# Written order for the second feed-forward product and a stepped final norm in a one-core encoder layer

## The chip, the cores and the metric

The kernel runs on 1 core of one Trainium2 chip. The metric is the device time of one execution in microseconds. Terms used below: TensorE (PE) multiplies matrices and writes to PSUM banks; VectorE (DVE), ScalarE (ACT) and GpSimd (POOL) work elementwise; SyncE (SP) here only starts transfers. Each engine has one queue and works through it in order. A transfer can be started from the queue of SP, ACT or POOL; only POOL's are used to add to what a tile holds.

## The reference

One layer of an encoder over 512 tokens of width 2048: a gated linear recurrence in both directions, differential attention, two gates, and a feed-forward part. The part that the change is about is the end:

```python
x = x + (g_m * branch_m + g_a * branch_a) @ w_out[l]
h2 = _rmsnorm(x, norm2_w[l])
gate, up = jnp.split(h2 @ w_ffn_in[l], 2, axis=-1)
x = x + (jax.nn.silu(gate) * up) @ w_ffn_out[l]      # 512 x 5632 times 5632 x 2048
return _rmsnorm(x, final_norm_w)
```

All of it is in float32.

## The kernel before

**Precision.** TensorE takes each float32 operand as a high and a low part (both of type float32r), and `mm3` issues three matmuls for a product: high by high, high by low, low by high. `split` makes the parts: ScalarE copies the source into the high part (line 149), VectorE subtracts it from the source to give the low part (line 150).

**Seven products for eight.** The large products are cut in 2 x 2 blocks and done by a scheme of seven multiplications with sums and differences of blocks (Strassen's, in Winograd's form). `seven` (line 335) writes one chunk. The inner dimension goes in groups g of 512. For every g the left side has seven factors (X11, S1, S2, X12, S3, S4, X22) and the right side (the weights) seven pieces of 128 x 1024: Q1, Q5, Q6, then Q2, Q3, Q7, then Q4. Some pieces are raw weight blocks, some sums that VectorE makes (lines 348, 356, 362, 369). One piece against one factor is a block of 12 matmuls of 128 x 128 by 512 columns.

**The second feed-forward product** is the chunks fo0 and fo1 (`fo_chunk`, line 1001), 1024 output columns each. The 11 groups of 512 are ten (0 to 9) by the scheme and one plain. The order of the work of a chunk is: first half, g = 0 to 9, each Q1, Q5, Q6 (raw blocks a, b, c); second half, g = 0 to 9, each Q2, Q3, Q7 (raw blocks d, f, e; in the last group f, e, d); the four plain pieces W12, W22, W11, W21, each against two factors; then ten Q4. That is 74 pieces and 78 blocks. Two PSUM banks each (i = 0, 1) of a, b and c collect the products, d those of the plain pieces. Q1, Q2 and the plain ones go to a; Q6, Q7, Q4 to b; Q5, Q3 to c.

**What feeds a block.** `take` (line 206) hands out piece n. Before that, `issue(n + AHEAD)` makes the parts of the pieces up to n + 2 and has `load` start the transfers of raw blocks up to eight further (SP's queue, line 197). There are 3 buffers for high parts, 3 for low parts, and 12 for raw blocks, 6 in a pool of their own and 6 of the 16 in `xpool`, where ten t2 sums live until Q4. The factors of the left side lie in DRAM since the first feed-forward product; `stream` (line 975) lists all 148 in order of use, fetches each with a GpSimd transfer four ahead (line 988) and makes its parts with `factor` (line 452). One such step is taken at each call of `work` (line 326), which `body` makes once per block. These tiles come from a pool of 39, `tpool`.

**After the products.** `post` of `added` (line 808) adds a finished bank into output tiles x of 128 x 512. Q1 gives three scaled copies on ScalarE for each bank (line 813); Q5 (816), Q6 (819), Q7 (821), D (826), Q3 (830), Q2 (834) and Q4 (837) add or subtract on VectorE. The residual x1 is added by a GpSimd transfer that accumulates from DRAM (line 802). `end` calls `final` (line 1002): ScalarE squares the tile and sums along the row (x2j, line 1004), VectorE multiplies by the norm's weight (line 1008) for three of the four tiles of a row block t. With the fourth, the sum of squares (1012) and the power (543, 544) give rstd, and the four tiles are scaled, two on ScalarE (1021), two on VectorE (1017, 1019), and stored (1022). Row blocks 0 and 1 end with Q2 of fo1, 2 and 3 with its Q4.

**What sets the order.** The program writes instructions into a list. `later(ns, fn)` holds a step back until a clock, which `tick` advances by 1296 per half block, has passed. From this list the framework's scheduler makes the five queues: it goes by written order as a priority and by its own estimate of when each operand and buffer is ready, so a queue's order may differ from the written one. Nothing is reordered while the kernel runs.

Of the kernel before, what the change touches and what calls it, by code (L numbers as in the profile page):

```python
# [12 lines left out]
F32 = mybir.dt.float32  # L13
# [7 lines left out]
P = 128  # L21
# [93 lines left out]
def build(ctx, tc, a, out):  # L115
# [12 lines left out]
    def ps(name):  # L128
        return pspool.tile([P, 512], F32, tag="ps", name=name)
# [44 lines left out]
    def parts(name, src, kt):  # L174
        n = src.shape[-1]
        hi = wpool.tile([P, n], F32R, tag="hi", name=f"whi_{name}")
        lo = wpool.tile([P, n], F32R, tag="lo", name=f"wlo_{name}")
        split(src, hi, lo)
        return tuple(w.rearrange("p (k c) -> p k c", k=kt) for w in (hi, lo))

    def chunk(name, srcs, kt, cols, body):
        first = len(pieces)
# [9 lines left out]
    def load(n):  # L192
        while len(raws) <= min(n, len(sources) - 1):
# [3 lines left out]
            nc.sync.dma_start(raw, src)  # L197
            raws.append(raw)

    def issue(n):  # L200
        while len(ready) <= min(n, len(pieces) - 1):
            name, need, make = pieces[len(ready)]
            load(need + (8 if sources[need][2] is not None else 6))
            ready.append(make(name))

    def take(it):
        n = next(it)
        issue(n + AHEAD)
        w = ready[n]
        ready[n] = None  # L210
        return w
# [110 lines left out]


    behind = []

    def work(must=False):
        if behind:
            ready_, fn = behind[0]
            while must and not ready_():
                tasks.pop(0)[1]()  # L330
            if ready_():
                behind.pop(0)
                fn()

    def seven(name, src, order, forms, post, start=None, plain=None, spare=False,
# [73 lines left out]
            add("Q4", g, len(sources) - 1, held(lambda g=g: t2[g]))  # L409

        def body(nm, it):
            bank = {k: [ps(f"{nm}_{k}{i}") for i in range(2)] for k in "abc"}
            last = {b_: n for n, (_, _, to, _) in enumerate(seq) for b_, _ in to}
            begun = set()
            for n, (q_, g, to, posts) in enumerate(seq):
                if start and g == order[0]:
                    start(q_)
                w = take(it)
                for b_, f_ in to:
                    if b_ not in bank:  # L420
                        bank[b_] = [ps(f"{nm}_{b_}{i}") for i in range(2)]
                    while f_ not in forms(g):
                        work(True)
                    hi, lo = forms(g)[f_]
                    for k in range(2):
                        for i in range(2):
                            sl = slice(i * P, (i + 1) * P)
                            mm3(bank[b_][i], [hi[:, k, sl], lo[:, k, sl]],
                                [w[0][:, k], w[1][:, k]], b_ not in begun and k == 0,
                                n == last[b_] and k == 1, skip=True)  # L430
                        yield 6 * MM
                    begun.add(b_)
                    if b_ != to[-1][0]:
                        work()
                for q_ in posts:
                    post(q_, bank)
                if during:
                    during(n)
                work()
# [12 lines left out]
    def factor(name, n, out, f_, src):  # L452

        if n:
            w = x_(f"{name}_{f_}", F32R)
            w = [w[:, :512], w[:, 512:]]
        else:
            w = [t_(f"{name}_{f_}{i}", F32R) for i in "hl"]
        w = tuple(x.rearrange("p (k c) -> p k c", k=2) for x in w)
        split(src, *w)  # L460
        out[f_] = w

    def kept(name, g, out, X, place=lambda n: n < 16):

        def s1():
            X["S"] = half(f"{name}_S")
            V.tensor_tensor(X["S"], X["X21"], X["X22"], ALU.subtract)
            factor(name, place(7 * g + 1), out, "S1", X["S"])

        def s2():  # L470
            V.tensor_tensor(X["S"], X["S"], X["X11"], ALU.subtract)
            factor(name, place(7 * g + 2), out, "S2", X["S"])

        def s3():
            V.tensor_tensor(X["X21"], X["X11"], X["X21"], ALU.subtract)
            factor(name, place(7 * g + 4), out, "S3", X["X21"])

        def s4():
            V.tensor_tensor(X["S"], X["S"], X["X12"], ALU.add)
            factor(name, place(7 * g + 5), out, "S4", X["S"])  # L480

        return ([lambda: factor(name, place(7 * g + 0), out, "X11", X["X11"]), s1, s2],
                [lambda: factor(name, place(7 * g + 3), out, "X12", X["X12"]), s4, s3,
                 lambda: factor(name, place(7 * g + 6), out, "X22", X["X22"])])
# [306 lines left out]
    def added(nm, n, src, final, plain=False):  # L791
# [16 lines left out]
        def post(q_, bank):  # L808
            a_, b_, c_ = (bank[k] for k in "abc")
            for i in range(2):  # L810
# [4 lines left out]
                elif q_ == "Q5":  # L815
                    V.tensor_tensor(x[22, i], x[22, i], c_[i], ALU.add)  # L816
                    G.dma_start(tile_(11, i), src(*place(11, i)))
                elif q_ == "Q6":
                    V.tensor_tensor(x[12, i], x[12, i], b_[i], ALU.subtract)
                elif q_ == "Q7":  # L820
                    V.tensor_tensor(x[22, i], x[22, i], b_[i], ALU.subtract)
                    if not plain:
                        fetch(22, i)
                        later(8000, lambda i=i: end(22, i))
                elif q_ == "D":
                    V.tensor_tensor(x[22, i], x[22, i], bank["d"][i], ALU.add)
                    fetch(22, i)
                    later(8000, lambda i=i: end(22, i))
                elif q_ == "Q3":
                    V.tensor_tensor(x[12, i], x[12, i], c_[i], ALU.add)  # L830
                    fetch(12, i)
                    later(8000, lambda i=i: end(12, i))
                elif q_ == "Q2":
                    V.tensor_tensor(x[11, i], x[11, i], a_[i], ALU.add)
                    end(11, i)
                else:
                    V.tensor_tensor(x[21, i], x[21, i], b_[i], ALU.add)  # L837
                    end(21, i)
        return post

# [81 lines left out]
    def fi_chunk(j):  # L922
# [39 lines left out]

        def start(q_):
            if q_ == "Q4" and j == NFB - 1:
                stream()
        order = (0, 1, 3, 2) if j == 0 else range(4)
        seven(f"fi{j}", lambda g, h_, l: a["w_ffi"][j, g, h_, l], order, lambda g: h2f[g], post,
# [7 lines left out]
    def stream():  # L975
# [20 lines left out]
            fetch(n)  # L996
        for m, g, _ in need:
            fgf[m, g] = {}
        when(lambda: True, [lambda n=n: make(n) for n in range(len(need))])

    def fo_chunk(n):
        def final(t, c, x):
# [4 lines left out]
            if len(mine) < 4:  # L1007
                later(0 if n else 30000, lambda: V.tensor_tensor(x, x, env["fnw"][c], ALU.mult))  # L1008
                tick(0)
                return  # L1010
            ss = sm("ss1", 1)
            V.tensor_reduce(ss, ss3p[:, t * 4:t * 4 + 4], AX.X, ALU.add)
            r = sm("rstd3", 1)
            pow_rstd(r, ss, D, 1)
            for k, (c, x) in enumerate(mine):
                if k == 3:
                    V.scalar_tensor_tensor(x, x, r, env["fnw"][c], ALU.mult, ALU.mult)
                elif k == 2:
# [1 line left out]
                else:  # L1020
                    A.activation(x, x, AF.Copy, scale=r)  # L1021
                (nc.sync if k > 1 else nc.scalar).dma_start(
                    out[t][:, c * 512:(c + 1) * 512], x)

        def start(q_):
            if q_ == "Q4" and n == 0:
# [432 lines left out]
    hm_split()  # L1459
    while chunks:  # L1460
        one()
    tick(1e9)


# [12 lines left out]
```

## Time and profile before

| | us |
|---|---|
| median of 3 runs | 2661.37 (2660.05 to 2668.32) |
| the profiled execution | 2664.15 |
| its span | 2662.4 |
| TensorE busy | 2599.0 (98% of the span) |
| VectorE busy | 2106.5 (79%) |
| ScalarE busy | 1308.8 (49%) |
| GpSimd busy | 253.7 (10%) |

The span runs from the first to the last instruction of the execution. All times in rows are from its start. A matmul's end is modelled from its size and matmuls overlap, so 0.39 us is shown for one where they start 0.23 us apart. PEclk is the mean clock granted to TensorE in a stretch, as a share of full speed. In rows that name a tile, buffer numbers are left out: fo_x is any output tile of fo0 or fo1, whi_fo_Q and wlo_fo_Q the high and low part of any piece, fs_ a streamed factor.

### The profile page before, as it was taken

What the parts mean: (1) busy time and instruction counts of PE and PEld (TensorE: products, weight loads), DVE (VectorE), ACT (ScalarE), POOL (GpSimd) and SP (SyncE); (2) the same over time, 40 slices, a digit from 0 to 9 for tenths busy, and PEclk for the clock granted to TensorE, in tenths of its full rate; (3) what the DMA queues carried; (4) which work ended last, traced back from release to release, by engine and by line L of the source; (5) the groups of instructions that cost most, each with busy time, mean ns of one, the idle gap of its engine ahead of it and who ended that gap; (6) DMA issues with size and microseconds to landing.
All of it is one profiled execution on the core that took longest, in us unless ns stands there. A gap on an engine that the chain in (4) does not pass through costs nothing. (4 is left out here: it accounts for less than half of the span.)

```text
span 2662.4 us, 33245 instructions
## 1 busy us (share of the span) xinstructions
PE 2599.0 (98%) x12184; PEld 2160.8 (81%) x12184; DVE 2106.5 (79%) x2660; ACT 1308.8 (49%) x1848; POOL 253.7 (10%) x448
## 2 busy tenths in 40 slices
PE   7999999999999999998999999999999999999997
PEld 6878888878889988887778888888888878787886
DVE  8977888788875675686788888788888879879885
ACT  8544444545543543354564444444444436646554
POOL 1000000011210122101200000000000001222211
PEclk9999999999999999999999999999999999999999
DMA  7655566744432345447755554565555577777763
GB/s 250 237 187 181 201 200 208 240 119 126 132 104 88 125 158 208 169 150 233 216 203 180 188 195 165 177 211 181 186 190 186 176 281 276 251 256 257 239 224 91
DMA packets 162227, 508.97 MB, mean 191 GB/s; under 512 B 21832, under 2 KB 22120, under 8 KB 162064
## 3 DMA queue, kind: packets, MB, share of 16 engines
q1 hardware_dynamic: 111456, 379.77, 41.6%
q0 software_dynamic: 33712, 97.71, 12.3%
q10 hardware_dynamic: 16896, 29.37, 3.2%
q8 instruction: 95, 1.56, 0.2%
q14 instruction: 68, 0.56, 0.1%
HBM read 445.41 MB, written 50.87 MB: 186 GB/s over the span
## 5 line engine op out<-in xcount | busy, mean ns | idle before, releaser
L145 PE MATMUL aqk_b<-xs,whi_aqk 128*128 128x512 f32 x512 | 161.6, 396 | 0.0
L149 ACT CAST whi_fi_Q<-fi_Q_t 128x1024 fp32r<-128x1024 f32 x88 | 92.5, 1052 | 116.7 <-PE fi_b L145 98.3
L145 PE MATMUL fi_a<-whi_fi_Q,h_X 128*128 128x512 f32 x440 | 147.2, 392 | 0.0
L145 PE MATMUL fi_c<-whi_fi_Q,h_S 128*128 128x512 f32 x440 | 144.6, 390 | 0.0
L145 PE MATMUL fi_b<-whi_fi_Q,h_S 128*128 128x512 f32 x352 | 115.6, 389 | 0.0
L145 PEld LDWEIGHTS aqk_b<-xs,whi_aqk 128*128 128x128 f32 x512 | 94.6, 189 | 18.3
L150 DVE TENSOR_TENSOR wlo_fi_Q<-fi_Q_t,whi_fi_Q 128x1024 fp32r<-128x1024 f32 x88 | 106.2, 1217 | 4.1 <-ACT whi_fi_Q L149 4.1
L362 DVE TENSOR_TENSOR raw_fi_e<-raw_fi_e,raw_fi_f 128x1024 f32<-128x1024 f32 x44 | 53.9, 1224 | 65.0 <-DMA raw_fi_e<-in_w_ffi 64.9
L145 PE MATMUL aqk_b<-xs,wlo_aqk 128*128 128x512 f32 x256 | 100.5, 393 | 0.0
L145 PEld LDWEIGHTS fi_c<-whi_fi_Q,h_S 128*128 128x128 f32 x440 | 82.6, 188 | 17.1
L145 PEld LDWEIGHTS fi_a<-whi_fi_Q,h_X 128*128 128x128 f32 x440 | 82.6, 188 | 16.8
L988 POOL DMA_DIRECT2D fs_X<-fg_X11d x22 | 11.8, 538 | 830.2 <-DVE wlo_fi_Q L150 785.5
L145 PE MATMUL fi_a<-wlo_fi_Q,h_X 128*128 128x512 f32 x220 | 86.0, 391 | 1.9 <-DVE wlo_fi_Q L150 1.8
L348 DVE TENSOR_TENSOR raw_fi_b<-raw_fi_b,raw_fi_a 128x1024 f32<-128x1024 f32 x44 | 53.8, 1223 | 41.5 <-DMA raw_fi_b<-in_w_ffi 36.7
L145 PE MATMUL fi_c<-wlo_fi_Q,h_S 128*128 128x512 f32 x220 | 86.0, 391 | 0.6 <-DVE wlo_fi_Q L150 0.5
L145 PE MATMUL ba_p<-whi_ba,hahl 128*128 128x512 f32 x256 | 82.5, 392 | 0.0
L149 ACT CAST whi_fi_Q<-raw_fi_e 128x1024 fp32r<-128x1024 f32 x44 | 46.4, 1055 | 73.1 <-PE fi_b L145 48.2
L149 ACT CAST whi_fi_Q<-raw_fi_b 128x1024 fp32r<-128x1024 f32 x44 | 46.5, 1056 | 69.5 <-PE fi_c L145 51.9
L145 PE MATMUL bm_p<-whi_bm,hmhl 128*128 128x512 f32 x256 | 80.5, 392 | 0.0
L145 PE MATMUL mqk_b<-xs,whi_mqk 128*128 128x512 f32 x256 | 80.4, 394 | 0.0
L149 ACT CAST whi_fi_Q<-raw_fi_f 128x1024 fp32r<-128x1024 f32 x44 | 46.4, 1055 | 67.4 <-PE fi_c L145 65.3
L145 PEld LDWEIGHTS fi_b<-whi_fi_Q,h_S 128*128 128x128 f32 x352 | 66.1, 188 | 13.6
(837 smaller groups left out, 8452.3 us busy)
## 6 DMA issues: line engine op xcount, KB each, us to landing
raw_fi_a<-in_w_ffi SPq DMA_DIRECT2D x44, 512.0 KB, 3.7
raw_fi_b<-in_w_ffi SPq DMA_DIRECT2D x44, 512.0 KB, 4.2
raw_fi_c<-in_w_ffi SPq DMA_DIRECT2D x44, 512.0 KB, 4.4
raw_fi_d<-in_w_ffi SPq DMA_DIRECT2D x44, 512.0 KB, 4.2
raw_fi_f<-in_w_ffi SPq DMA_DIRECT2D x44, 512.0 KB, 3.8
raw_fi_e<-in_w_ffi SPq DMA_DIRECT2D x44, 512.0 KB, 4.2
raw_aqk<-in_w_aqk SPq DMA_DIRECT2D x32, 512.0 KB, 3.6
raw_fo_a<-in_w_ffo SPq DMA_DIRECT2D x20, 512.0 KB, 4.8
```

The lines of the kernel that those rows point to most:

```text
L145: T.matmul(dst, lhs[l], rhs[r], start=first and i == 0, stop=last and i == 2, skip_group_check=skip)
L149: A.copy(hi, src)
L150: V.tensor_tensor(lo, src, hi.bitcast(F32), ALU.subtract)
L348: V.tensor_tensor(raws[r12], raws[r12], raws[r11], ALU.add)
L362: V.tensor_tensor(raws[r12], raws[r12], raws[r22], ALU.add)
L988: G.dma_start(got[n], fgd[g][f_].rearrange("p (k c) -> p k c", k=2))
```

## The change

From the first block of fo0 to the end, everything is put in a `manual_schedule` region: there each engine issues its instructions in written order. To suit that, the written order changes. A low part is written one piece after its high part: `parts` returns a function for it and `take` calls that one piece ahead (in the region) or as soon as before (outside; there only the order of the low part and of the t2 sum of a Q2 piece changes). A factor's low half is written at the next `work`. `post` is held back by 2000 (two half blocks) in the region. `stream` makes a factor only when it is at most five ahead of the factors used. The last Q4 piece of a chunk goes through its two output banks one after the other instead of in turn. Q4's two additions are written ahead of both `end` calls. The final norm is cut in steps that `later` spreads: for row blocks 0 and 1 by 1300 each, for 2 and 3 by 1. The steps left over are written in their order at the end.

```diff
     def parts(name, src, kt):
         hi = wpool.tile([P, n], F32R, tag="hi", name=f"whi_{name}")
-        lo = wpool.tile([P, n], F32R, tag="lo", name=f"wlo_{name}")
-        split(src, hi, lo)
-        return tuple(w.rearrange("p (k c) -> p k c", k=kt) for w in (hi, lo))
+        A.copy(hi, src)
+
+        def low():
+            lo = wpool.tile([P, n], F32R, tag="lo", name=f"wlo_{name}")
+            V.tensor_tensor(lo, src, hi.bitcast(F32), ALU.subtract)
+            return tuple(w.rearrange("p (k c) -> p k c", k=kt) for w in (hi, lo))
+        return low
...
+    region = []
+
+    def written():
+        if not region:
+            region.append(ctx.enter_context(tc.manual_schedule()))
+
+    def behindhand(fn):
+        if region:
+            later(2000, fn)
+        else:
+            fn()
...
     def take(it):
         n = next(it)
         issue(n + AHEAD)
+        while lows[0] < min(len(ready), n + (2 if region else 3)):
+            ready[lows[0]] = ready[lows[0]]()
+            lows[0] += 1
...
     def work(must=False):
+        if low_parts:
+            low_parts.pop(0)()
         if behind:
...
         def body(nm, it):
+            if nm == "fo0":
+                written()
...
+                used[0] += len({(g, f_) for _, f_ in to} - met)
+                met |= {(g, f_) for _, f_ in to}
                 w = take(it)
...
-                    for k in range(2):
-                        for i in range(2):
+                    for h_ in range(2):
+                        for j in range(2):
+                            k, i = (j, h_) if plain and n == len(seq) - 1 else (h_, j)
...
                 for q_ in posts:
-                    post(q_, bank)
+                    behindhand(lambda q_=q_: post(q_, bank))
...
     def factor(name, n, out, f_, src):
-        split(src, *w)
-        out[f_] = w
+        A.copy(w[0], src)
+
+        def low():
+            V.tensor_tensor(w[1], src, w[0].bitcast(F32), ALU.subtract)
+            out[f_] = w
+        if region:
+            low_parts.append(low)
+        else:
+            low()
...
                     V.tensor_tensor(x[21, i], x[21, i], b_[i], ALU.add)
+            if q_ == "Q4":
+                for i in range(2):
                     end(21, i)
...
-        when(lambda: True, [lambda n=n: make(n) for n in range(len(need))])
+        for n in range(len(need)):
+            when(lambda n=n: n < used[0] + 5, [lambda n=n: make(n)])
...
         def final(t, c, x):
-            ss = sm("ss1", 1)
-            V.tensor_reduce(ss, ss3p[:, t * 4:t * 4 + 4], AX.X, ALU.add)
+
             r = sm("rstd3", 1)
-            pow_rstd(r, ss, D, 1)
-            for k, (c, x) in enumerate(mine):
+
+            def scale():
+                ss = sm("ss1", 1)
+                V.tensor_reduce(ss, ss3p[:, t * 4:t * 4 + 4], AX.X, ALU.add)
+                pow_rstd(r, ss, D, 1)
+
+            def put(k):
+                c, x = mine[k]
...
+            step = 1300 if t < 2 else 1
+            later(step * (1 + t % 2), scale)
+            for k in (0, 3, 1, 2):
+                later(step * (3 + 4 * (t % 2) + (0, 2, 3, 1)[k]), lambda k=k: put(k))
...
-    tick(1e9)
+    while tasks:
+        tasks.pop(0)[1]()
```

## Rows read from the trace of the kernel before

**Rows 1.** Windows: width, busy (x count) of PE, PEld, DVE, ACT, POOL; PEclk, DMA share, GB/s

```profile
2290.00:2372.00 82.00, 78.89 (x342) 63.38 (x341) 73.24 (x83) 49.77 (x67) 20.51 (x39) 1.00 0.89 312
2372.00:2421.50 49.50, 46.40 (x199) 36.93 (x199) 34.40 (x42) 21.52 (x34) 11.05 (x18) 1.00 0.70 218
...
2507.00:2616.00 109.00, 107.52 (x472) 88.04 (x472) 86.01 (x96) 59.40 (x79) 25.21 (x43) 1.00 0.68 215
2616.00:2652.00 36.00, 31.94 (x132) 25.41 (x130) 19.03 (x27) 16.29 (x27) 1.12 (x2) 0.95 0.16 58
sum 445.40, PE 432.57 PEld 351.76 DVE 372.09 ACT 248.50 POOL 88.77; mean PE 72.09 PEld 58.63 DVE 62.02 ACT 41.42 POOL 14.79
```

**Rows 2.** Tiles fo_a, fo_b (min/median/max ns, first to last start) and one chain piece

```profile
L145 PE MATMUL fo_a<-whi_fo_Q,fs_X11h x80: 389/389/477, 2206.6 to 2506.6; 128*128 128x512 f32 x80
...
L145 PE MATMUL fo_b<-whi_fo_Q,fs_X22l x80: 387/389/628, 2398.6 to 2651.7; 128*128 128x512 f32 x80
...
2516.58 2.72 PE fo_c L145 x12
```

**Rows 3.** Waits of TensorE from 2180 on: us in total, times, longest

```profile
PE fo_b L145 <- DVE wlo_fo_Q L150: 4.6, 8, 0.8
```

**Rows 4.** Waits of VectorE, SP's timeline 2478 to 2500, one piece of the chain

```profile
DVE raw_fo_e L362 <- DMA raw_fo_e<-in_w_ffo: 11.4, 9, 2.8
...
2479.66 1.46 SPq L197 DMA_DIRECT2D raw_fo_d<-in_w_ffo  x2
2485.41 0.33 SPq L197 DMA_DIRECT2D raw_fo_e<-in_w_ffo  x1
2490.34 0.33 SPq L197 DMA_DIRECT2D raw_fo_f<-in_w_ffo  x1
2494.35 0.33 SPq L197 DMA_DIRECT2D raw_fo_e<-in_w_ffo  x1
...
2494.35 5.02 DMA raw_fo_e<-in_w_ffo
```

**Rows 5.** Timelines of ScalarE and VectorE around 2400: start, us, what, idle before

```profile
2395.77 0.63 ACT L1004 ACTIVATE x2j<-fo_x 128x512 f32<-128x512 f32 x1 [7.24 <-DMA fo_x<-x1d]
...
2401.51 1.23 DVE L150 TENSOR_TENSOR wlo_fo_Q<-fo_Q_t,whi_fo_Q 128x1024 fp32r<-128x1024 f32 x1 [9.48 <-ACT whi_fo_Q L149]
```

**Rows 6.** Timelines of ScalarE and TensorE around 2630, and a window after it

```profile
2629.23 2.94 ACT L149 CAST whi_fo_Q<-fo_Q_t 128x1024 fp32r<-128x1024 f32 x3 [0.41 <-ACT fo_x L1021]
...
2630.33 0.73 PE L145 MATMUL fo_b<-whi_fo_Q,fs_X22h 128*128 128x512 f32 x2 [3.53 <-ACT whi_fo_Q L149]
...
2631.00:2636.00 5.00, 4.47 (x13) 3.54 (x13) 2.80 (x3) 1.43 (x3) 0.00 (x0) 0.66 0.27 101
```

**Rows 7.** VectorE's timeline in fo0's first half; tile fo_x: the scalings of Q1

```profile
2221.05 0.68 DVE L150 TENSOR_TENSOR fs_S1l<-fs_S,fs_S1h 128x512 fp32r<-128x512 f32 x1
2221.66 1.21 DVE L150 TENSOR_TENSOR wlo_fo_Q<-raw_fo_a,whi_fo_Q 128x1024 fp32r<-128x1024 f32 x1
2222.79 0.68 DVE L150 TENSOR_TENSOR fs_S2l<-fs_S,fs_S2h 128x512 fp32r<-128x512 f32 x1
...
L813 ACT ACTIVATE fo_x<-fo_a x12: 593/612/647, 2284.0 to 2509.2; 128x512 f32<-128x512 f32 x12
```

**Rows 8.** Tile x1d from 2200 on: its transfers

```profile
DMA to landing us min/median/max: 3.9/5.5/8.3
```

**Rows 9.** Tile fo_x: last additions and stores; ScalarE's timeline from 2652 on

```profile
L837 DVE TENSOR_TENSOR fo_x<-fo_x,fo_b x4: 680/685/689, 2432.3 to 2652.1; 128x512 f32<-128x512 f32 x4
...
L1022 ACTq DMA_DIRECT2D out<-fo_x x8: 338/338/375, 2626.2 to 2657.3; - x8
...
2653.87 1.33 ACT L1021 ACTIVATE fo_x<-fo_x,rstd 128x512 f32<-128x512 f32 x2 [0.35 <-POOL rstd L544]
```

**Rows 10.** Waits of GpSimd from 2200 on; tile fs_S: its transfers

```profile
POOL fs_X L988 <- DVE fs_S4l L150: 24.2, 9, 4.2
...
DMA to landing us min/median/max: 2.8/4.9/10.7
```

More of the change, by code (lines that the diff above doesn't have):

```diff
@@ L198, in load @@
             raws.append(raw)
+    region = []
[7 more added lines that the diff above has]
+            fn()
+    lows = [0]
     def issue(n):
@@ L324, in build @@
     behind = []
+    used = [0]
+    low_parts = []
     def work(must=False):
+        if low_parts:
+            low_parts.pop(0)()
         if behind:
@@ L414, in body @@
             begun = set()
+            met = set()
             for n, (q_, g, to, posts) in enumerate(seq):
@@ L459, in factor, with flush @@
         w = tuple(x.rearrange("p (k c) -> p k c", k=2) for x in w)
-        split(src, *w)
-        out[f_] = w
+        A.copy(w[0], src)
[6 more added lines that the diff above has]
+            low()
+    def flush():
+        while low_parts:
+            low_parts.pop(0)()
     def kept(name, g, out, X, place=lambda n: n < 16):
@@ L470, in s2 @@
         def s2():
+            flush()
             V.tensor_tensor(X["S"], X["S"], X["X11"], ALU.subtract)
@@ L478, in s4 @@
         def s4():
+            flush()
             V.tensor_tensor(X["S"], X["S"], X["X12"], ALU.add)
@@ L964, in start @@
             if q_ == "Q4" and j == NFB - 1:
+                used[0] = -4
                 stream()
```

## The prediction, made before the change was run

> **What bounds the kernel now.** The page's engine shares put TensorE far ahead, so only its stalls can be won. The diff gives written order from the second feed-forward product (chunks fo0 and fo1) to the end, so I cut that stretch into windows and compared each width with TensorE's busy time [rows 1]. It idles 3.1 us in fo0's second half, 3.1 us around fo0's last pieces, 1.5 us in fo1's second half and after, and 4.1 us in fo1's last pieces. In all 445.4 - 432.6 = 12.8 us are idle, so the two first halves, which are not shown, are nearly dense.
>
> The loss is larger than the idle time. A block of twelve matmuls takes 2.72 us in a dense run [rows 2]. Each chunk has 78 blocks (70 of the seven products, 8 of the W pieces), so the two need 156 x 2.72 = 424.3 us. From the first fo matmul at 2206.6 to the last at 2651.7 there are 445.1 us [rows 2], and eight transposes in between cost about 1. So about **20 us** are lost: the 12.8 us of idle time, the restarts (a matmul after a wait shows 0.39 us where the dense rate is 2.72/12 = 0.23), and slow matmuls below.
>
> The waits say what comes late. Eight waits of the b bank's matmuls are for a low part, wlo_fo_Q, 0.8 us at most [rows 3]. Behind these VectorE waits 11.4 us for raw_fo_e to land [rows 4]. That transfer is late because its buffer was spoken for: the loads went out as d, d, e, f, e, where the pieces are used d, f, e [rows 4]; the e of 2494.35 went out just before its use, and the chain of waits runs through its 5.02 us [rows 4]. Around fo0's last pieces ScalarE stands still for 7.24 us ahead of a square, x2j, whose operand is still being accumulated by a transfer; the next whi_fo_Q stands behind four squares, and VectorE's low part waits 9.48 us for it [rows 5]. In fo1's last pieces six squares and four scalings of the final norm stand ahead of a whi_fo_Q, which starts at 2629.23; TensorE waits 3.53 us, then runs at a granted share of 0.66 (part of it at 1.2 instead of 2.4 GHz) over the next 5 us [rows 6].
>
> **The change, part by part.**
>
> *Loads in written order.* No instruction is added. SP then loads d, f, e in order of use, each ten pieces before its product. Five of the six buffers of either pool are taken by such a lead, and the sixth came free some three pieces earlier, so a raw piece has about 20 us to land where the late one took 5.02 [rows 4]. The waits for raw_fo_e and raw_fo_f go, and with them the idle time of fo0's second half and part of fo1's.
>
> *Low parts one piece ahead in place of two.* VectorE's order within a step becomes sum for piece n+2, low part of n+1, posts, low half of a factor. Back to back, a low part occupies it 1.13 us and a factor half 0.61 [rows 7]; a sum has the low part's shape, so I price it alike. Three pieces with their two sums and three halves need 5 x 1.13 + 3 x 0.61 = 7.5 us, against 3 x 2.72 = 8.16 of TensorE: it keeps up, with 8% spare. The high part of n+2 may start when block n-1 has freed its buffer; about 1.0 us later (three in a row take 2.94) [rows 6] the low part may follow, and it is wanted two blocks after that start: 5.44 - 1.0 - 1.13 = 3.3 us of slack, as before.
>
> *Where written order still bunches work.* (a) At the change from a chunk's first half to its second, ScalarE gets six scalings of 0.62 [rows 7] among its copies, and VectorE four additions of 0.6. Walking both queues from the end of the last Q1 block (0): the high part of Q2 ends at 1.1, the scalings at 4.4, the next two high parts at 6.0 and 7.6; VectorE does two additions (to 4.1), a half (5.6), a sum (6.7), a low part (7.9), two additions (9.2), a half and a sum (11.0), and the low part of Q7 (12.1). That is wanted at 4 x 2.72 + 0.2 = 11.1: a stall of 1.0, twice. (b) In fo1's Q4 pieces four multiplications by fnw, chained to squares, and two additions are written between two low parts; the second ends at 7.2 where 5.6 was wanted: 1.5. (c) At fo0's start the tail of the first product is unchanged: 0.6. With 0.3 per restart that is about **5 us left**.
>
> *Squares.* They are now emitted seven half-blocks after their transfer. In real time that is W11 and W21 (10.9 us) and a high part (1.1) after W22's end, so 12 us. The transfers start within 3 us of that end and take 3.9 to 8.3 us [rows 8], so they land 7 to 11 us after it. I take no wait. Bounds: nothing, or the 7.24 us again, of which 3.1 us of idle time [rows 1] and about five restarts of 0.3 reached TensorE, 4.6 in all. The Trainium skill (Perfetto Trace Analysis, Tensor Engine Instruction) calls the queues of ACT, DVE and GpSimd strict FIFO: an entry not ready holds all behind it. The rows of the squares agree. By that rule one late transfer brings the old stall back, which is rival B.
>
> *Final norm in steps.* For rows 0 and 1 the reductions and scalings are spread over ten half-blocks of fo1's Q4; 4 x (0.7 + 0.34) = 4.2 us of ScalarE [rows 9] lie in 13.6 us, where the copies leave about 5 idle. The stall there goes: 4.1 us idle [rows 1], 1.7 from 5 us at 0.66 [rows 6] and two restarts, 6.4 in all.
>
> *The tail.* From the last addition (2652.1) to the end are 10.3 us [rows 9]. The last piece now finishes one output tile half a block early, so its addition and square are done when the other tile ends, and the second reduction no longer stands behind scalings: about 1 us earlier. Against this, each ScalarE scaling (0.67 apart now) has its transfer's issue written right behind it, so four scalings and four issues run one by one: 1.7 + 4 x 1.1 = 6.1 us after the last bank, where the last issue now ends 5.5 after it [rows 9]. I take +0.3, ends -0.7 and +0.8. The Trainium skill (Perfetto Trace Analysis, DMA Instruction, HWDGE) has the sequencer wait for such an issue's semaphore before it goes on; no row shows an issue between two scalings, and without that rule the tail would be 0.5 shorter.
>
> *Before the region.* Only the order of low part and sum in Q2's pieces changes. The sum needs no high part and about fits in the wait for it (1.0 us against 1.13), so nothing; if the cover is gone, the nearest row is a short wait for a low part, 0.8 us, a few times. I take 0, ends -3 and +3.
>
> *Sum.* 20 - 5 = 15 lost microseconds return, less 0.3 of the tail and rounded down to **14** for small stalls not walked. The profiled execution took 2664.15 us (span 2662.4), 2.8 above the median of 2661.37; it would take about 2650.2, and the median 2661.37 - 14 = **2647.4**.
>
> **The rivals.**
>
> *A, the forecast* (0.62): 2644 to 2653.
>
> *B, the wait moves* (0.16): squares or a factor's copy still stand ahead of high parts in ScalarE's written order. For it: 5.5 us is the median transfer, 8.3 the longest [rows 8]. Against: the later emission. The 4.6 us of the squares and three more stalls of 1.0 stay: 14 - 7.6 = 6.4 gained, 2655.
>
> *C, slower* (0.10): the factor stream is now held to five ahead, so a fetch is emitted four steps, 10.9 us, before its copy. GpSimd waits up to 4.2 us for a buffer, and a transfer lands in 4.9 us typically, 10.7 at worst [rows 10]. If the sum passes 10.9, ScalarE waits, and all behind it. It decides from 14/148 = 0.1 us per factor on; at 0.25 us it costs 37, and the median would be 2684. Against: 4.2 + 4.9 = 9.1 leaves 1.8 us, and fewer factors alive leave more buffers free.
>
> *D, it does nothing* (0.04): the waits were the transfers' rate, not their order; 2661. For it: a DMA share of 0.89 in fo0's second half [rows 1]. Against: 0.68 in fo1's, with the same loads.
>
> *E, all stalls go* (0.08): 20 less, 2641.
>
> **How the numbers follow.** A change of 0.3% (8 us) is about what a measurement here can tell. A, E and the better part of B lie below 2653.4: 0.74. The rest of B and D lie within it: 0.16. C gives 0.10. The range runs from E's 2641 less one to D with its 3 us, 2640 to 2664.
>
> **What would show it.** Right: loads in the order d, f, e; no wait of VectorE for raw_fo_e; the chain of waits almost all TensorE; no stall over 1.5 us from fo0 on; granted clock 1.00 to the last block; a tail of about 10.6 us. Wrong: ScalarE waiting for transfers (x2j or fs tiles), idle time of TensorE in the first halves, or VectorE never waiting while TensorE does.

## The result, and the profile after

| | before | after |
|---|---|---|
| median, four runs each on the same chip (us) | 2660.71 (2657.53 to 2668.32) | 2642.15 (2639.95 to 2643.95) |
| the profiled execution; its span | 2664.15; 2662.4 | 2642.52; 2639.6 |
| first and last fo matmul start | 2206.6, 2651.7 | 2198.6, 2628.8 |
| from the first to the last: **the stretch** | 445.1 | 430.3 |
| of it, beyond the dense pitch of matmuls: **lost** | 19.2 | 5.1 |
| last fo matmul to the end: **the tail** | 10.72 | 10.75 |

"Lost" sums what the steps from one matmul's start to the next take beyond the dense 0.227 us, over the steps that are longer by more than 0.05.

The changed kernel is faster: ratio 0.9926 (95% interval 0.9911 to 0.9940), 18.6 us by the medians where 14 were forecast. The traces say where it comes from. Their spans differ by 2662.4 - 2639.6 = 22.8 us. Of these the stretch gives 445.1 - 430.3 = 14.8, and the tail nothing. The remaining 2206.6 - 2198.6 = 8.0 us lie ahead of fo0, where all five engines have the same instructions in the same order in both kernels, but for some two dozen of VectorE's and nine of SP's in the last 26 us; 7.0 of the 8.0 are there before these.

The windows over the same parts of the work as in [rows 1] (their edges do not fall on exactly the same matmuls), from fo0's second half on; the columns are those of [rows 1]:

```profile
2282.00:2364.00 82.00, 81.42 (x359) 67.09 (x359) 77.67 (x85) 47.52 (x61) 19.98 (x38) 1.00 0.93 319
2364.00:2413.50 49.50, 49.50 (x221) 40.96 (x220) 32.08 (x38) 26.16 (x42) 13.20 (x22) 1.00 0.54 160
2413.50:2498.00 84.50, 83.19 (x367) 68.60 (x366) 81.77 (x92) 51.31 (x71) 17.00 (x31) 1.00 0.76 268
2498.00:2600.00 102.00, 101.42 (x447) 83.64 (x447) 86.74 (x96) 52.96 (x68) 22.17 (x39) 1.00 0.69 219
2600.00:2628.60 28.60, 27.56 (x121) 22.44 (x120) 19.58 (x28) 17.09 (x29) 2.52 (x3) 1.00 0.23 83
```

Width less TensorE's busy time is 0.6, 0.0, 1.3, 0.6 and 1.0 us. Around fo0's last pieces nothing is idle any more, and the granted clock is 1.00 up to the last block. The DMA share of fo0's second half rose from 0.89 [rows 1] to 0.93 while its idle time went from 3.1 to 0.6: the rate of the transfers was not the limit there, so rival D's reason falls.

The waits of TensorE in the stretch, and VectorE's three largest up to the last fo matmul (us in total, times, longest):

```profile
PE fo_b L145 <- DVE wlo_fo_Q L181: 2.2, 3, 1.0
PE fo_c L145 <- DVE wlo_fo_Q L181: 1.3, 1, 1.3
```

```profile
DVE wlo_fo_Q L181 <- ACT whi_fo_Q L177: 23.6, 32, 3.0
DVE fs_X22l L497 <- ACT fs_X22h L494: 13.1, 6, 3.0
DVE fo_x L1059 <- ACT x2j L1055: 4.9, 1, 4.9
```

VectorE waits for no transfer at all; the 11.4 us for raw_fo_e [rows 4] are gone. Its largest wait is now for ScalarE's high parts, 23.6 us in 32 waits, but TensorE waits only four times for a low part, 3.5 us in all. These four, from its timeline (start, us, what, idle before and its releaser):

```profile
2288.00 0.50 PE L145 MATMUL fo_b<-wlo_fo_Q,fs_S3h 128*128 128x512 f32 x1 [0.58 <-DVE wlo_fo_Q L181]
...
2425.61 0.50 PE L145 MATMUL fo_c<-wlo_fo_Q,fs_S1h 128*128 128x512 f32 x1 [1.31 <-DVE wlo_fo_Q L181]
...
2502.64 0.50 PE L145 MATMUL fo_b<-wlo_fo_Q,fs_S3h 128*128 128x512 f32 x1 [0.58 <-DVE wlo_fo_Q L181]
...
2607.35 0.50 PE L145 MATMUL fo_b<-wlo_fo_Q,fs_X22h 128*128 128x512 f32 x1 [1.04 <-DVE wlo_fo_Q L181]
```

The shown matmul runs on 0.39 us into the idle time, so from start to start these are 0.97, 1.70, 0.97 and 1.43 us instead of 0.23: 0.74, 1.47, 0.74 and 1.20 beyond the pitch. The first and third are the changes of halves, the fourth is fo1's Q4, all where the prediction put them. The second, at fo1's start, it did not have.

### The profile page after: what moved, and what is told of

Read it like the earlier page. It is cut to its first block, busy times and chain, and to the rows that moved or that the text cites. A ratio compares the mean times of both kernels' runs of the same rounds, so it can differ in the third digit from the quotient of the medians.

```text
span 2639.6 us, 33237 instructions
## 1 busy us (share of the span) xinstructions
PE 2590.0 (98%) x12184; PEld 2158.8 (82%) x12184; DVE 2106.2 (80%) x2660; ACT 1308.3 (50%) x1848; POOL 255.1 (10%) x448
## 3 DMA queue, kind: packets, MB, share of 16 engines
q0 software_dynamic: 33712, 97.71, 12.1%
## 4 chain that ended last, share of the span: by engine, by line
PE 77%; DVE 10%; DMA 6%; issue 4%; ACT 2%; POOL 0%; ACTq 0%; DVEq 0%; SPq 0%; POOLq 0%
PE fi_b L145 12%; PE fi_c L145 8%; PE fi_a L145 8%; PE fo_b L145 6%; PE aqk_b L145 5%; PE fo_a L145 4%; PE fo_c L145 4%; PE mqk_b L145 3%; PE bm_p L145 3%; PE ba_p L145 3%; PE mv_p L145 3%; PE ga_b L145 2%; PE gm_b L145 2%; PE ga_a L145 1%; PE ga_c L145 1%
## 5 line engine op out<-in xcount | busy, mean ns | idle before, releaser
L145 PEld LDWEIGHTS aqk_b<-xs,whi_aqk 128*128 128x128 f32 x512 | 94.1, 188 | 17.9
L145 PEld LDWEIGHTS fi_c<-whi_fi_Q,h_S 128*128 128x128 f32 x440 | 83.0, 189 | 17.3
```

What stands on the lines that cost most here:

```text
L145: T.matmul(dst, lhs[l], rhs[r], start=first and i == 0, stop=last and i == 2, skip_group_check=skip)
```

## The experiments

Each kernel was profiled once; "total" is its median (six runs for x1 and x9) or single time. First fo matmul, stretch, lost and tail are measured as in the table above.

| run | total | first fo | stretch | lost | tail |
|---|---|---|---|---|---|
| x1 the changed kernel again | 2646.98 | 2207.1 | 430.3 | 5.2 | 10.75 |
| x2 before, SP alone in written order | 2655.41 | 2200.6 | 442.3 | 16.9 | 10.73 |
| x3 before, all engines in written order | 2723.69 | 2199.2 | 510.8 | 83.8 | 11.98 |
| x4 after, ordered by the scheduler | 2665.19 | 2205.4 | 447.3 | 21.3 | 10.75 |
| x5 after, SP ordered by the scheduler | 2647.09 | 2204.3 | 430.3 | 5.1 | 10.75 |
| x6 after, low part beside high part | 2708.00 | 2202.4 | 493.1 | 65.6 | 10.76 |
| x7 after, norm not in steps | 2659.03 | 2206.7 | 438.7 | 13.6 | 11.81 |
| x8 after, squares early | 2648.44 | 2205.1 | 430.8 | 5.7 | 10.76 |
| x9 after, fnw spread, stores from SP | 2644.46 | 2206.0 | 428.3 | 3.1 | 10.76 |
| x10 after, posts not held back | 2644.40 | 2197.3 | 434.3 | 9.1 | 10.75 |
| x11 after, short factor stream | 2652.05 | 2208.2 | 431.3 | 6.0 | 10.80 |
| x12 after, old order of the tail | 2645.12 | 2200.3 | 430.3 | 5.1 | 10.97 |

Where four of the kernels lose it (us, by first half, second half, and plain pieces with Q4 of each chunk):

| | fo0 first | fo0 second | fo0 rest | fo1 first | fo1 second | fo1 rest |
|---|---|---|---|---|---|---|
| before | 0.72 | 4.53 | 4.46 | 0.99 | 2.29 | 6.18 |
| after | 0.55 | 0.85 | 0 | 1.58 | 0.85 | 1.31 |
| x2 | 2.12 | 1.10 | 3.58 | 0.78 | 2.46 | 6.84 |
| x4 | 0.77 | 8.16 | 9.13 | 0 | 3.03 | 0.17 |

**Is the part ahead of fo0 chance?** x1 is the changed kernel, unaltered.

> The changed kernel once more. Of the 22.8 us between the two traces, 14.9 lie between the first and the last fo matmul (445.1 to 430.3) and 8.0 ahead of the first (2206.6 to 2198.6), where all five queues are the same instruction by instruction. Theory: the 8.0 are chance, the stretch is the change. Then the stretch is 430 again within 1 us, the first fo matmul lies anywhere from 2196 to 2208, and the ratio is 0.993 to 0.995. Rival: the program ahead of fo really became faster (buffers, semaphores); then the first fo matmul is at 2198 or 2199 again and the ratio stays at 0.9926 or below.

Measured: ratio 0.9930 (0.9910 to 0.9950), six runs against eleven. The stretch is 430.3 again, while the first fo matmul starts at 2207.1 instead of 2198.6. Over the runs of the table that start spreads from 2197.3 to 2208.2, with the same instructions ahead of it up to the last 26 us or so. So the 8.0 us are chance in the main; single totals carry about 11 us of it, and the experiments are judged by stretch and tail. One thing stays open. By the means the total falls by 19.8 us in the runs of the result and by 17.9 in those of x1, 3 to 5 more than the stretch. The intervals are wide (16 to 24 and 13 to 24 us), but the kernel before was traced only once, so whether its stretch is always 445 us is not known; the stretch of the changed kernel came as 430.3 in both its traces.

**The order of the loads, or of the other engines?** x2 takes the kernel before and puts SP alone in written order:

```diff
         def body(nm, it):
+            if nm == "fo0":
+                ctx.enter_context(tc.manual_schedule(
+                    engines={mybir.EngineType.SP}))
```

> The kernel before, with SP's queue alone in written order from fo0 on. Theory (order of the loads): the waits for raw_fo_e and raw_fo_f go, and the 3.1 us of idle time of fo0's second half with some 2 of fo1's; squares and norm stay late. First to last fo matmul about 440 of 445. Rival (rate of the transfers): 444 to 446, with VectorE still waiting for raw_fo_e.

x5 is the opposite: the changed kernel, whose region holds every engine but SP.

```diff
-            region.append(ctx.enter_context(tc.manual_schedule()))
+            region.append(ctx.enter_context(tc.manual_schedule(engines={
+                mybir.EngineType.PE, mybir.EngineType.Activation,
+                mybir.EngineType.DVE, mybir.EngineType.Pool})))
```

> The changed kernel with SP left to the scheduler: its loads go out in another order (d, f, d, f, e, d, e, f at the start of a second half), the other four queues as written. With SP alone in written order the waits for raw_fo_e stayed, and the sum of e and f stood 25 us ahead of its use in VectorE's queue, against 2.5 in the changed kernel. Theory (the place of the sum, not the order of the loads, made the late wait): first to last fo matmul 430 to 431, no wait of VectorE for raw_fo_e or raw_fo_b over 1 us. Rival (the order of the loads): 432 to 436, with such waits back.

x2 loads in the order d, f, e, and VectorE still waits for the transfers; its stretch, 442.3, lies between the two expectations. Its waits in x2:

```profile
DVE raw_fo_b L348 <- DMA raw_fo_b<-in_w_ffo: 13.0, 7, 3.5
DVE raw_fo_e L362 <- DMA raw_fo_e<-in_w_ffo: 9.7, 7, 4.2
```

x5's loads are out of order, d, f, d, e (SP's timeline in x5):

```profile
2461.68 0.58 SPq L201 DMA_DIRECT2D raw_fo_d<-in_w_ffo  x1
2469.93 0.33 SPq L201 DMA_DIRECT2D raw_fo_f<-in_w_ffo  x1
2474.81 0.33 SPq L201 DMA_DIRECT2D raw_fo_d<-in_w_ffo  x1
2475.19 0.42 SPq L201 DMA_DIRECT2D raw_fo_e<-in_w_ffo  x1
```

Yet no wait for a transfer is among VectorE's, and the stretch is 430.3. In sum the order of the loads is worth the 2.8 us of x2 (one trace each), and nothing once the rest is in order. The mechanism of the prediction holds in one place: in fo0's second half x2 wins back 3.4 of the 3.7 us that the change does. In fo1's it wins nothing, with a wait of 4.2 us there, and fo0's first half loses 1.4 more. So the order of the loads is not what the waits rest on. What differs between the kernels with them and those without, the tile raw_fo_e shows: the load, the sum of e and f, and the copy that uses the sum (durations, then first and last start), before:

```profile
L197 SPq DMA_DIRECT2D raw_fo_e<-in_w_ffo x20: 327/328/423, 2241.3 to 2558.0; - x20
L362 DVE TENSOR_TENSOR raw_fo_e<-raw_fo_e,raw_fo_f x20: 1212/1225/1228, 2252.9 to 2561.7; 128x1024 f32<-128x1024 f32 x20
L149 ACT CAST whi_fo_Q<-raw_fo_e x20: 1043/1048/1057, 2290.1 to 2583.6; 128x1024 fp32r<-128x1024 f32 x20
```

and after:

```profile
L201 SPq DMA_DIRECT2D raw_fo_e<-in_w_ffo x20: 327/328/1197, 2249.5 to 2537.9; - x20
L390 DVE TENSOR_TENSOR raw_fo_e<-raw_fo_e,raw_fo_f x20: 1214/1217/1219, 2281.5 to 2562.9; 128x1024 f32<-128x1024 f32 x20
L177 ACT CAST whi_fo_Q<-raw_fo_e x20: 1052/1056/1057, 2282.9 to 2565.4; 128x1024 fp32r<-128x1024 f32 x20
```

Before, the first sum stands 37 us ahead of its use, the last 22; after, 1.4 and 2.5. Over all twenty, paired one to one, the median is 25.4 before and 2.5 after, and from a load's issue to its sum 5.3 against 27.1 us. In x2 they are 25.1 and 6.2, in x5 2.5 and 26.7. So the loads were not late for the product. The sum stands about 5 us behind its load's issue, close to where the transfer lands (median 4.4 us, at most 8.9), and low parts that TensorE wants soon stand behind it. VectorE's timeline before, and the matmul that waited:

```profile
2499.46 1.23 DVE L362 TENSOR_TENSOR raw_fo_e<-raw_fo_e,raw_fo_f 128x1024 f32<-128x1024 f32 x1 [2.81 <-DMA raw_fo_e<-in_w_ffo]
2500.61 1.22 DVE L150 TENSOR_TENSOR wlo_fo_Q<-fo_Q_t,whi_fo_Q 128x1024 fp32r<-128x1024 f32 x1
...
2501.88 0.50 PE L145 MATMUL fo_b<-wlo_fo_Q,fs_S2h 128*128 128x512 f32 x1 [0.60 <-DVE wlo_fo_Q L150]
```

That the engines' order other than SP's does it is shown; that it is this place in VectorE's queue is read from the waits and leads of four traces, since no run moves the sum alone.

x4 asks for the rewritten program without the region:

```diff
-            region.append(ctx.enter_context(tc.manual_schedule()))
+            region.append(None)
```

> The changed text, without the region: low parts, held posts, stream limit? no: those that hang on the region fall back to the form of before, the stream's limit, the stepped norm and the tail stay, and the scheduler orders all queues. Theory: loads are out of order again and squares late, the norm's stall (6.4) is gone: first to last fo matmul about 438, VectorE waiting for raw_fo_e. Rival (the text does it, the region nothing): 430 to 432.

Here the expectation described the edit wrongly in part: since the list is not empty, low parts one piece ahead, held posts and the limit of the stream stay as well, and only the ordering falls to the scheduler. It gives 447.3: the rewritten text alone gains nothing in sum. The old waits are back, VectorE's 12.1 us for raw_fo_e and ScalarE's 16.1 us for accumulated tiles. The steps of the norm work here too: from fo1's plain pieces on 0.2 us is lost, where it was 6.2 before. But fo0's second half and last pieces lose 17.3 instead of 9.0, with one wait of 3.74 us.

**The low part in a second step.** x3 gives the kernel before the region and no rewriting; x6 writes the changed kernel's low part right behind its high part.

```diff
         def body(nm, it):
+            if nm == "fo0":
+                ctx.enter_context(tc.manual_schedule())
```

> The kernel before, with every engine in written order from fo0 on and the text not rewritten. Theory (region and rewriting both needed): loads cured, but posts stand right behind their block and the final norm in one piece ahead of a copy, so first to last fo matmul 436 to 440. Rival 1 (the region does it all): 430 to 432. Rival 2 (posts at once hold up VectorE every time): over 445.

```diff
-        while lows[0] < min(len(ready), n + (2 if region else 3)):
+        while lows[0] < min(len(ready), n + 3):
```

> The changed kernel with the low part of a piece written right behind its high part, as before, and all else as in the change. The region alone took 510.8 us from first to last fo matmul. Theory (the low part in a second step is what makes written order pay): behind a sum the low part must wait some 1.1 us for ScalarE's copy; 40 of the sums per chunk, with two waits to three pieces, need 7.5 + 2.2 = 9.7 us where TensorE needs 8.16, so 40 to 60 us more: 470 to 490. Rival (the region alone lost by its posts and the norm in one piece): 430 to 436.

The region alone costs 510.8 - 445.1 = 65.7 us, far more than was expected (436 to 440; the rival of over 445 had put it on the posts). Without the second step the changed kernel takes 493.1 - 430.3 = 62.8 us more. VectorE's timeline in fo0's first half of x6 shows why, and under it one row of ScalarE's:

```profile
2244.10 1.23 DVE L181 TENSOR_TENSOR wlo_fo_Q<-raw_fo_b,whi_fo_Q 128x1024 fp32r<-128x1024 f32 x1 [1.19 <-ACT whi_fo_Q L177]
2245.24 0.68 DVE L497 TENSOR_TENSOR fs_S2l<-fs_S,fs_S2h 128x512 fp32r<-128x512 f32 x1
2245.84 1.22 DVE L384 TENSOR_TENSOR fo_Q_t<-raw_fo_b,raw_fo_c 128x1024 f32<-128x1024 f32 x1
2248.25 1.23 DVE L181 TENSOR_TENSOR wlo_fo_Q<-fo_Q_t,whi_fo_Q 128x1024 fp32r<-128x1024 f32 x1 [1.19 <-ACT whi_fo_Q L177]
...
2254.14 1.23 DVE L181 TENSOR_TENSOR wlo_fo_Q<-raw_fo_b,whi_fo_Q 128x1024 fp32r<-128x1024 f32 x1 [1.19 <-ACT whi_fo_Q L177]
```

```profile
2247.17 1.05 ACT L177 CAST whi_fo_Q<-fo_Q_t 128x1024 fp32r<-128x1024 f32 x1 [2.58 <-DVE fo_Q_t L384]
```

The sum ends, ScalarE copies it, and VectorE stands still for that copy, because the low part is its next instruction; ScalarE in turn stands still while VectorE is on its way to the next sum. Three pieces take 2254.14 - 2244.10 = 10.04 us, where TensorE's three blocks take 8.16. VectorE's work alone was 7.5 in the prediction; the two idle times of 1.19 bring it to 9.9.

**The written steps one at a time.** x10 calls `post` at once, x8 has the squares of accumulated tiles follow at the next tick, x7 writes the final norm in one piece:

```diff
-                    behindhand(lambda q_=q_: post(q_, bank))
+                    post(q_, bank)
```

> The changed kernel with each post written right behind its last block, not two half blocks later. Theory: VectorE reaches the post about a block before TensorE is done with the bank and waits with the next low parts behind it; a few posts per chunk, each eating 1 to 2 us of 3 us of slack: 432 to 436 from first to last fo matmul, the stalls at the change of halves grown. Rival (the slack takes it all): 430 to 431.

```diff
-                        later(8000, lambda i=i: end(22, i))
+                        later(1 if region else 8000, lambda i=i: end(22, i))
...
-                    later(8000, lambda i=i: end(22, i))
+                    later(1 if region else 8000, lambda i=i: end(22, i))
...
-                    later(8000, lambda i=i: end(12, i))
+                    later(1 if region else 8000, lambda i=i: end(12, i))
```

> The changed kernel with the squares of the accumulated tiles written one half block after their transfer is started, in place of seven. Theory: ScalarE stands still until the transfer has landed (7 to 11 us after W22 in fo0) and the high parts of the Q4 pieces stand behind it: a stall of 1 to 4 us in fo0, less in fo1, so 431 to 435. Rival (the high parts ahead of it are enough, the distance was not needed): 430 to 431.

```diff
-            later(step * (1 + t % 2), scale)
-            for k in (0, 3, 1, 2):
-                later(step * (3 + 4 * (t % 2) + (0, 2, 3, 1)[k]), lambda k=k: put(k))
+            scale()
+            for k in range(4):
+                put(k)
```

> The changed kernel with the final norm of a row block written in one piece again. Theory: ScalarE gets two squares, two waits for rstd, four scalings and four issues (about 7 us) ahead of the next high part, which has 3 us of slack: a stall of 3 to 4 us in fo1's Q4 pieces and slow matmuls after it, so 434 to 437 from first to last fo matmul, granted clock under 1 near the end. Rival (any order hides it): 430 to 431.

Posts at once cost 434.3 - 430.3 = 4.0 us, nearly all in one place. VectorE does wait 12.3 us for the d banks in x10, but TensorE has no stall there. The loss is at fo1's start: Q4's additions wait for the b bank, then six multiplications by the norm's weight stand ahead of a low part. VectorE's timeline in x10, and TensorE's:

```profile
2411.08 0.69 DVE L884 TENSOR_TENSOR fo_x<-fo_x,fo_b 128x512 f32<-128x512 f32 x1 [1.61 <-PE fo_b L145]
...
2417.65 3.70 DVE L1059 TENSOR_TENSOR fo_x<-fo_x,fnw 128x512 f32<-128x512 f32 x6
...
2424.28 0.80 PE L145 MATMUL fo_a<-wlo_fo_Q,fs_X11h 128*128 128x512 f32 x1 [2.47 <-DVE wlo_fo_Q L181]
```

The 4.0 are thus the price of early posts together with this block of six; what posts alone cost no run shows. The squares' distance is worth 0.5. ScalarE waits 9.2 us for accumulated tiles in x8, as much as the 9.3 of the kernel before, but in eight waits of at most 2.7 us where before it was two of up to 7.2; all but 0.5 is hidden. The steps of the norm are worth 8.4 in the stretch and 1.1 in the tail, more than the 4 to 7 expected. x7 has the old stall back, longer: TensorE's timeline there, and two windows behind it.

```profile
2622.02 0.79 PE L145 MATMUL fo_b<-wlo_fo_Q,fs_X22h 128*128 128x512 f32 x1 [7.50 <-DVE wlo_fo_Q L181]
2622.61 0.63 PE L145 MATMUL fo_b<-whi_fo_Q,fs_X22l 128*128 128x512 f32 x1
```

```profile
2622.00:2626.60 4.60, 4.58 (x11) 3.63 (x12) 3.74 (x5) 3.51 (x5) 0.00 (x0) 0.54 0.67 260
2626.60:2631.00 4.40, 4.40 (x21) 3.63 (x20) 2.72 (x4) 3.03 (x4) 0.00 (x0) 1.00 0.00 0
```

After 7.5 us of idle time the granted clock is 0.54 (nearly all at 1.2 of 2.4 GHz) for 4.6 us, in which 11 matmuls start; at the dense pitch it would be 20. That is about 2 us on top of the stall.

**The factor stream.** x11 moves towards rival C: the stream three ahead in place of five, its fetches two ahead in place of four.

```diff
-            when(lambda n=n: n < used[0] + 5, [lambda n=n: make(n)])
+            when(lambda n=n: n < used[0] + 3, [lambda n=n: make(n)])
...
-            fetch(n + 4)
+            fetch(n + 2)
```

> The changed kernel with the factor stream cut to three ahead and its fetches to two ahead of their copy. For rival C of the prediction (the shorter stream makes ScalarE wait): a fetch then leads by about two blocks, 5.4 us, where a transfer takes 4.9 typically and 10.7 at worst, so ScalarE waits at many of 148 factors and the stretch grows to 440 or more. Against it: the factor's three steps of lead still hide most, 430 to 434; then rival C was far off.

It costs 1.0 us in all. With half the lead four fetches come late, and ScalarE waits 9.0 us for them, 3.3 at most, but nearly all of it is hidden; at the lead of the change no such wait is left. Rival C had no footing.

**The tail, and a version that might beat both.** x12 takes back the order of the two output banks and the additions ahead of `end`. x9 spreads fo0's and fo1's multiplications by fnw over half blocks and issues all stores from SP.

```diff
-                            k, i = (j, h_) if plain and n == len(seq) - 1 else (h_, j)
+                            k, i = h_, j
...
-            if q_ == "Q4":
-                for i in range(2):
-                    end(21, i)
+                    end(21, i)
```

> The changed kernel with the last piece's two output banks in turn again and each end right behind its addition. Theory: the stretch stays at 430.3; the first addition can start 0.7 us later against the last matmul, so square and rstd of the first row block come 0.7 later, and the tail grows from 10.75 by 0.5 to 0.7. Rival (the serial scalings and issues on ScalarE set the tail): within 0.2 of 10.75.

```diff
-                later(0 if n else 30000, lambda: V.tensor_tensor(x, x, env["fnw"][c], ALU.mult))
+                spread[0] += 1
+                later(2600 if n else 12000 + 2592 * spread[0],
+                      lambda: V.tensor_tensor(x, x, env["fnw"][c], ALU.mult))
...
-                (nc.sync if k > 1 else nc.scalar).dma_start(
+                nc.sync.dma_start(
```

> The changed kernel with three edits for what is left: fo0's multiplications by the norm's weight spread over its Q4 pieces (six in a row, 3.7 us, stood ahead of the low part of fo1's fourth piece: a stall of 1.5), fo1's written two half blocks later (a stall of 1.2), and all stores started from SP, so that ScalarE's four last scalings run back to back. Theory: first to last fo matmul 430.3 less 2.5, 427.8; tail 10.75 less 1.2, 9.5; ratio to the kernel before 0.992, 3 to 4 us under the changed kernel. Rival for the tail (the landing of the last store sets it, wherever it is started): tail 10.5 or more.

x12's tail is 10.97, so the reordering is worth 0.2 us, not the 0.5 to 0.7 expected. x9's stretch is 428.3, the shortest of all: the stall at fo1's start is gone, the one in fo1's Q4 fell from 1.43 to 0.79. Its ratio, 0.9923 (0.9907 to 0.9938), can't be told from the 0.9930 of x1. Its tail did not move, where 9.5 was expected. ScalarE's timeline at the end of the changed kernel:

```profile
2630.86 0.72 ACT L1077 ACTIVATE fo_x<-fo_x,rstd 128x512 f32<-128x512 f32 x1 [0.15 <-POOL rstd L591]
2631.61 0.34 ACTq L1078 DMA_DIRECT2D out<-fo_x  x1
2631.99 0.72 ACT L1077 ACTIVATE fo_x<-fo_x,rstd 128x512 f32<-128x512 f32 x1 [0.42 <-ACT fo_x L1077]
...
2635.02 0.36 ACTq L1078 DMA_DIRECT2D out<-fo_x  x1
```

ScalarE's and SP's timelines at the end of x9:

```profile
2636.33 2.69 ACT L1079 ACTIVATE fo_x<-fo_x,rstd 128x512 f32<-128x512 f32 x4 [0.15 <-POOL rstd L591]
...
2637.08 4.46 SPq L1080 DMA_DIRECT2D out<-fo_x  x8
```

And all of x9's stores in the view of the output (ns min/median/max, first and last start):

```profile
L1080 SPq DMA_DIRECT2D out<-fo_x x16: 332/384/604, 2615.2 to 2640.9; - x16
```

With an issue between them, scalings start 2631.99 - 2630.86 = 1.13 us apart; in x9 four take 2.69. The Trainium skill (Perfetto Trace Analysis, DMA Instruction, HWDGE) says that the sequencer is free for its next instruction only when it is through with such an issue, and the 1.13 agrees with that. But eight issues on SP take 4.46 us and grow from 0.33 to 0.60 each, so from the first scaling the last issue ends 2637.08 + 4.46 - 2636.33 = 5.2 us on, where it was 2635.02 + 0.36 - 2630.86 = 4.5 before. The transfers land a little sooner after their issue (the last in 3.1 us in place of 3.5), and the tail comes out even.

## Why the prediction was right, and where it was not

**The sum** held: 14 of the stretch were forecast (20 lost, 5 left), 14.8 came (19.2 lost, 5.1 left). The time alone would not have told: 2642.15 lies nearer to rival E's 2641, and it is the 5.1 us still lost that decide for the forecast. The median's 18.6 is this and 3.8 us more. Chance ahead of fo0, where single traces spread by 11 us, can give so much; that it did is not shown. In two places the sum came right in part by luck, as *Loads in written order* and *Stalls left* say below.

***Loads in written order*** is the step that failed. "Late because its buffer was spoken for" carries fo0's second half at most, where x2 gives back 3.4 us. Over both chunks x2 cures the order and keeps the waits, and x5 leaves the order and loses them. The sum of e and f stood 25 us early on VectorE's queue. The idle time of fo1's second half returned all the same, because the region puts VectorE's queue in order along with SP's: there the number was right from the wrong cause.

***Low parts one piece ahead*** was priced at nothing ("3.3 us of slack, as before"). The slack is there, but the step is the condition for all the rest: 62.8 us without it (x6). The prediction walked the new order alone and never the old order under the region; that would have shown the slower case, of which rival C, in another place, was no picture.

***Squares***: no wait reached TensorE, as taken (4.5 us lost around fo0's last pieces before, 4.6 by the prediction, none after), but not because of the seven half blocks, which x8 shows to be worth 0.5. Rival B's wait does come back in x8 (9.2 us on ScalarE). Its single waits of up to 2.7 us are shorter than the 3.3 us of slack that the prediction walked, which would hide them; that this is the reason is argued, not shown.

***Final norm in steps***: right in place, mechanism and size. The 6.4 forecast as lost there were 6.2 in the kernel before. x7's 8.4 is larger because under written order the undivided norm stalls TensorE for 7.5 us instead of 3.5, and it costs 1.1 of the tail as well. The posts, held back, were not priced; early posts cost 4.0 in x10, together with the block of six below.

***Stalls left***: the places were right, the sizes too large. Beyond the pitch, 1.0 twice at the change of halves measured 0.74 twice; 1.5 in fo1's Q4 measured 1.20; 0.6 at fo0's start measured 0.24. The 0.3 per restart came from no row: 0.39 us is shown for every matmul, not only behind a wait, and behind these stalls the next one starts 0.34 us on instead of 0.23, which is 0.11. The forecast for these four stalls with their restarts was 5.3, and they came to about 3.4. That the total is 5.1 is luck, because 1.47 at fo1's start was missed: six multiplications by fnw, due after their 30000, stand as one block on VectorE ahead of the sum and the low part. The timeline of VectorE after:

```profile
2418.99 3.69 DVE L1059 TENSOR_TENSOR fo_x<-fo_x,fnw 128x512 f32<-128x512 f32 x6
...
2424.34 1.22 DVE L181 TENSOR_TENSOR wlo_fo_Q<-raw_fo_b,whi_fo_Q 128x1024 fp32r<-128x1024 f32 x1
```

***The tail***: +0.3 forecast, 0.0 measured. The serial scalings and issues came as walked: the last issue ends 6.1 us after the last addition starts. But the last store then lands 3.5 us after its issue, where it took 4.1 before. The early tile gives 0.2 (x12), not "about 1 us". Taking the issues off ScalarE does not save the 0.5 either: x9 does it and keeps the tail, with SP's issues in their place.

Not settled: how the 65.7 us of x3 divide between the low parts, the posts and the norm, which overlap there; what the place of the sum alone is worth; and the 3 to 5 us by which the totals fall more than the stretch.

## What to carry to other kernels

When an engine waits for a transfer, look at the place of the waiting instruction in its queue before the transfer's: if the result is used only 25 us later, as here, the order is the first suspect, and the work behind the wait is what suffers. Written order paid here only once the two halves of a hand-over between engines were written a step apart; the same region on unchanged text cost 66 us. Judge a change of one stage by that stage in the trace: equal queues ahead of it spread by 11 us, against a gain of 15.

## What the runs showed that was not expected

The clock behind two short stalls: in x10 TensorE's gap of 2.86 us is followed by a granted 0.64 (2424.3 to 2429, part of it at 1.2 of 2.4 GHz), with matmuls 0.43 us apart; behind the changed kernel's gap of 1.70 us it is 1.00 and they start 0.23 apart.

Eight issues that followed one another on SP's queue grew from 0.33 to 0.60 us (x9), and gathering all stores on the idle engine did not shorten the end. The cause is not shown: with the stores on two queues, in the changed kernel, one of SP's issues there took 1.00 us.

Two engines that hand each other every piece can lose a fifth of the pace with both well under full: in x6 three pieces take 10.04 us, where TensorE needs 8.16 and VectorE's work is 7.5.
